# A two-layer encoder trunk: the residual of the feed-forward part moved to DRAM for two of three down products

## The chip, the cores and the metric

The kernel runs on one core of one Trainium2 chip. The metric is the device time of one execution in microseconds (us); lower is better. Three runs of the kernel before gave 1168.78, 1169.61 and 1171.22 us, so the median is 1169.61 us. One more execution was recorded by the hardware profiler, and all rows in this document come from such recorded executions.

## What is computed

Two layers act on a residual stream `x` of 512 tokens by 1024 features, in fp32. Each layer does a token mixer beside a cross-attention, an output projection that is added to `x`, and then the feed-forward part that this change is about:

```python
h = rms_norm(x, ffn_norm[i])
u = h @ w_up                       # 1024 -> 2 * 2816
c = causal_depthwise_conv(u) + b   # width 3
a, g = split(c)
x = x + (silu(g) * a) @ w_down     # 2816 -> 1024
```

The first layer's mixer is differential attention, the second's is a gated linear attention.

## The kernel before, in words

**Layout.** The residual is held transposed: features on the 128 partitions, 512 tokens along the free axis. It has eight tiles `xT[0..7]` of 128x512, stored in pairs as four `xpair` tiles of 128x2x512 in a pool with tag `x2` that has 16 buffers. The same 16 buffers hold the normalised activations `xh`, `xl` (eight pairs: each fp32 operand is split in a rounded high part and a low remainder, and three matmuls take the place of one) and the operands `t1`, `b11` of the down products. Small work tiles of 128x512 come from a second pool with tag `xs` that has five buffers (`xtile()`, line 168).

**Feed-forward part** (`ffn`, line 1106). There are 22 up steps, each of which makes 128 columns of `a` and 128 columns of `g` on TensorE, applies the convolution (ScalarE and VectorE), SiLU (ScalarE) and the product (VectorE), and makes operands of the down product. `GROUPS` = (3, 4, 4) says how many pairs of up steps go into a down product, so the down product is done in three groups; groups one and two stand between up steps, and group three ends the layer. `_ffn()` (line 47) writes this order out: 7 up steps, group one, 8 up steps, group two, 7 up steps, group three.

**A down group** (`down`, line 1154) is written in Strassen's way as 14 products ("steps") with weights `a11`, `s1`, `a12`, `s2`, `s4`, `s3`, `a22` for each of two column halves `c`. A step has 18 matmuls of 128x256 in group one and 24 in the others (3 or 4 blocks, two column tiles, three terms). The result of a step stays in a PSUM bank with tag `lg`, `tp` or `mm` (two banks each), and later steps of the same half go on accumulating in the same bank: `s2`, `s3` and `a22` in the `lg` bank of `a11`, `s4` in the `tp` bank of `s1`. After each step but before the next one in its bank, the bank's content is added to a quarter of the residual: `add(c, tag, f, t)` (line 1176) adds it to the 256 tokens `t` of `xpair[2 * c + f]`. This is one VectorE instruction on 128x512 values, line 1178, that reads PSUM and the residual and writes the residual. Over the 14 adds, the (half, f, t) quarters in order are: c = 0: (0,0), (1,1), (0,0), (0,1), (0,1), (1,1); c = 1: (0,0); c = 0: (1,0); c = 1: (1,1), (0,1), (0,0), (1,1), (0,1), (1,0).

**Weights.** All weights are loaded by SyncE (SP) from one packed tensor into `raw` tiles of which there are six (line 236). ScalarE rounds each to `whi` (line 227 for up weights, 263 for down weights), VectorE subtracts to get `wlo` (lines 230 and 265); there are five buffers of each. VectorE also makes the Strassen sums of the raw down weights (lines 247 to 255). `prefetch` (line 289) keeps the made weights up to five blocks ahead of the matmuls.

**Order of the work.** TensorE follows the order of the program text throughout. Inside a down group ScalarE, VectorE and GpSimd (POOL) follow it too; elsewhere, and for SP always, a scheduler orders the instructions when the kernel is built, by its own forecast of when each is ready. A buffer is given out again when its last reader is done, a DMA included. The kernel reserves 1024 bytes per partition for the descriptors of DMAs that GpSimd issues (line 1337), and issues none from GpSimd in the kernel before. In layer one, the last down group also settles the residual for the next layer and stores it to `xres` in DRAM (line 1239), from which it is read back late in layer two (line 1061); in layer two it stores the output.

Of the kernel before, what the change touches and what calls it, by code (L numbers as in the profile page):

```python
# [11 lines left out]
F32 = mybir.dt.float32  # L12
# [3 lines left out]
ALU = mybir.AluOpType  # L16
# [5 lines left out]
S = 512  # L22
KT = D // 128
# [7 lines left out]
GROUPS = (3, 4, 4)  # L31
X2, XS, EM = 16, 5, 7
# [14 lines left out]
def _ffn():  # L47

    steps, q = [], 0
    for i, nq in enumerate(GROUPS):  # L50
        steps += [("up", t) for t in range(2 * q + (i > 0), 2 * (q + nq) + (i + 1 < len(GROUPS)))]
        steps.append(("down", i))
        q += nq
    return steps
# [96 lines left out]
def trunk(ctx, tc, head_d, x_t, mem_t, wpack, cols_a_d, cols_d, conv_d, gate_d, rel_bias, diff_lambda, consts, onehot, out):  # L151
    nc = tc.nc
    mm = nc.tensor.matmul
    V, A, G = nc.vector, nc.scalar, nc.gpsimd

    perm = ctx.enter_context(tc.tile_pool(name="perm", bufs=1))
    xs = ctx.enter_context(tc.tile_pool(name="xs", bufs=1))
# [3 lines left out]
    dr = ctx.enter_context(tc.tile_pool(name="dr", bufs=1, space=DRAM))  # L161
    ctx.enter_context(tc.manual_schedule(engines={mybir.EngineType.PE}))

    def bank(tag):
        return ps.tile([128, 512], F32, name=f"ps_{tag}", tag=tag)

    def xtile():
        return xs.tile([128, S], F32, name="xt", tag="xs", bufs=XS)
# [14 lines left out]
    def blk(b, w=128):  # L183
        return slice(w * b, w * b + w)
# [13 lines left out]
    def tables(name):  # L198
        tc.keep_in_program_order(A.preload_act_table_set(name))
# [89 lines left out]
    def prefetch(i):  # L289
        size = lambda j: 1 if plan[j][0][0] == "d" else len(blocks[j])  # L290
        by_block = plan[i][0][0] in "ud"
        while len(made) <= i or (len(made) < len(plan) and (
                sum(map(size, range(i, len(made) + 1))) <= WB if by_block else len(made) < i + 2)):
            make_piece()

    def weights(key, more=True):
        i = used[0]
        assert plan[i][0] == key, (plan[i][0], key)
        if more:
            prefetch(i)  # L300
        used[0] += 1
        parts, made[i] = made[i], None
        return parts
# [49 lines left out]
    xT, xpair = [None] * KT, [None] * (KT // 2)  # L353
    xh, xl = [None] * KT, [None] * KT
    xres = dr.tile([KT, 128, S], F32, name="xres")
    bias_d = dr.tile([6, 640], F32, name="bias_d")
    cols_a = perm.tile([128, 32], F32, name="cols_a")
    cols = perm.tile([128, 26], F32, name="cols")
# [76 lines left out]
    with tc.tile_pool(name="ini", bufs=1) as ip, tc.manual_schedule(engines={E.Activation, E.DVE, E.Pool, E.SP}):  # L435
# [7 lines left out]
        p = bank("tp")  # L443
# [662 lines left out]
    def ffn(pool, l, acc):  # L1106
# [47 lines left out]
        def down(g, mids, finish):  # L1154
            last, ks = len(mids) - 1, tuple(range(len(mids)))
            parts, banks, first, last_group = {}, {}, used[0], g + 1 == len(GROUPS)

            def step(c, tag, w, m, ks=ks, start=False, more=True):
                if (c, w) not in parts:
                    parts[c, w] = weights(("d", l, g, c, w), more)  # L1160
                elif more:
                    prefetch(first + more)
                if start:
                    banks[c, tag] = bank(tag)
                p = banks[c, tag]
                hi, lo = parts[c, w]
                for k in ks:
                    mh, ml = mids[k][m]
                    for n in range(2):
                        o, ws = p[:, blk(n, 256)], slice(256 * k + 128 * n, 256 * k + 128 * n + 128)  # L1170
                        terms = (hi, mh), (hi, ml), (lo, mh)
                        for i, (a, b) in enumerate(terms):
                            mm(o[:, ::-1], a[:, ws], b[:, ::-1], start=start and (k, n, i) == (0, 0, 0), stop=k == last and i == 2,  # L1173
                               skip_group_check=True)

            def add(c, tag, f, t):
                x = xpair[2 * c + f][:, :, blk(t, 256)]
                V.tensor_add(x, x, banks[c, tag].rearrange("p (n s) -> p n s", n=2))  # L1178

            def done(c, f, t=None):  # L1180
                for n in range(2):
                    finish(4 * c + 2 * f + n, t)
            if not last_group:
                step(0, "lg", "a11", "b11", start=True)
                add(0, "lg", 0, 0)
                step(0, "tp", "s1", "t1", start=True)
                add(0, "tp", 1, 1)
                step(0, "mm", "a12", "b21", start=True)
                add(0, "mm", 0, 0)
            else:  # L1190
                step(0, "lg", "a11", "b11", ks[:-1], True)
                step(0, "tp", "s1", "t1", ks[:-1], True, False)
                step(0, "mm", "a12", "b21", ks[:-1], True, False)
                step(0, "lg", "a11", "b11", ks[-1:], more=False)
                add(0, "lg", 0, 0)
                step(0, "tp", "s1", "t1", ks[-1:], more=1)
                add(0, "tp", 1, 1)
                step(0, "mm", "a12", "b21", ks[-1:], more=2)
                add(0, "mm", 0, 0)
            step(0, "lg", "s2", "t2")  # L1200
            add(0, "lg", 0, 1)
            step(0, "tp", "s4", "b22")
            add(0, "tp", 0, 1)
            step(0, "lg", "s3", "t3")
            add(0, "lg", 1, 1)
            step(1, "lg", "a11", "b11", start=True)
            add(1, "lg", 0, 0)
            step(0, "lg", "a22", "t4")
            add(0, "lg", 1, 0)
            done(0, 0)  # L1210
            step(1, "tp", "s1", "t1", start=True)
            add(1, "tp", 1, 1)
            step(1, "lg", "s2", "t2")
            add(1, "lg", 0, 1)
            done(0, 1)
            if l == 0 and last_group:
                tables("natural_log_exp_and_others")
            step(1, "mm", "a12", "b21", start=True)
            add(1, "mm", 0, 0)
            done(1, 0, 0)  # L1220
            step(1, "lg", "s3", "t3")
            add(1, "lg", 1, 1)
            done(1, 1, 1)
            step(1, "tp", "s4", "b22")
            add(1, "tp", 0, 1)
            done(1, 0, 1)
            step(1, "lg", "a22", "t4")
            add(1, "lg", 1, 0)
            done(1, 1, 0)
# [11 lines left out]
        def first_steps():  # L1241
            both = [[weights(("u", l, i, h)) for h in range(2)] for i in range(2)]
            banks = [[bank(t) for _ in range(2)] for t in ("mm", "sm")]
            old = list(zip(xh, xl))
            for ks in (K8[:4], K8[4:]):
                for i in range(2):
                    for h in range(2):
                        product(banks[i][h], both[i][h], 0, old, ks)
                        if (i, h, ks[0]) == (0, 1, 0):
                            row_scales(acc[0])  # L1250
                for n in ks[:2]:
                    scaled(n)
                if ks[0]:
                    rows(banks, 0)
                for n in ks[2:]:
                    scaled(n)
            rows(banks, 1)
            return banks
# [6 lines left out]
                banks[i][h] = t[:, blk(h, S)]  # L1265

        opened = None
        for what, i in _ffn():
            if what == "up":
                if i == 0:  # L1270
                    opened = first_steps()
                if i < 2:
                    us = opened[i]
                else:
                    us = [bank("mm" if i % 2 == 0 else "sm") for _ in range(2)]
                    for h in range(2):
                        product(us[h], weights(("u", l, i, h)), 0, list(zip(xh, xl)))
                prefetch(used[0])
                ca = conv(us[0], i)
                cg = conv(us[1], 22 + i)  # L1280
                A.activation(cg, cg, AF.Silu)
                if i % 2 == 0:
                    w = pool.tile([128, 8, 256], F32, name="w", bufs=1)
                    mids.append({})
                V.tensor_mul(w[:, 1 + 2 * (i % 2):3 + 2 * (i % 2)].rearrange("p a b -> p (a b)"), ca, cg)
                middle(i % 2, w, mids[-1])
            else:
                n, last = GROUPS[i], i == len(GROUPS) - 1
                with tc.manual_schedule(engines={E.Activation, E.DVE, E.Pool}):
                    down(i, mids[:n], finish if last else lambda n, t: None)  # L1290
                mids = mids[n:]
# [90 lines left out]
```

## Time and profile before

| what | us |
|---|---|
| median of three runs | 1169.61 |
| the profiled execution, its own time | 1169.78 |
| its span, first to last instruction | 1167.9 |
| TensorE (PE) busy | 1153.8 |
| weight loads into TensorE (PEld) busy | 986.4 |
| VectorE (DVE) busy | 886.4 |
| ScalarE (ACT) busy | 598.9 |
| GpSimd (POOL) busy | 4.1 |

The profiled execution took 1.88 us more than its span. Busy times are sums of the recorded durations of an engine's instructions, overlaps counted once. Matmuls are pipelined, so their recorded durations overlap; how fast TensorE goes is read from the distance of their starts. The feed-forward part of layer one lies at about 256 to 607 us of the span, that of layer two at about 812 to 1168 us. Down groups one and two are at 333 to 363 and 450 to 490 us in layer one and at 890 to 920 and 1007 to 1047 us in layer two.

A row of the table by stages reads: window, its length, then for each engine its busy time and (xcount) of instructions, then the granted TensorE clock as a share of full speed, the mean busy share of the 16 DMA engines, and GB/s moved. A row of a list by source line reads: line, engine, operation, out<-in, count, duration in ns as min/median/max, first and last start. A row of DMA issues reads: out<-in, queue, count, KB each, and the median us from issue to landing. A row of waits reads: who waited <- for whom: us in total, times, the longest. "q" behind an engine's name is its instruction queue, so SPq is SyncE's, which issues DMAs.

### The profile page before, as it was taken

What the parts mean: (1) busy time and instruction counts of PE and PEld (TensorE: products, weight loads), DVE (VectorE), ACT (ScalarE), POOL (GpSimd) and SP (SyncE); (2) the same over time, 40 slices, a digit from 0 to 9 for tenths busy, and PEclk for the clock granted to TensorE, in tenths of its full rate; (3) what the DMA queues carried; (4) which work ended last, traced back from release to release, by engine and by line L of the source; (5) the groups of instructions that cost most, each with busy time, mean ns of one, the idle gap of its engine ahead of it and who ended that gap; (6) DMA issues with size and microseconds to landing.
All of it is one profiled execution on the core that took longest, in us unless ns stands there. A gap on an engine that the chain in (4) does not pass through costs nothing.

```text
span 1167.9 us, 16705 instructions
## 1 busy us (share of the span) xinstructions
PE 1153.8 (99%) x6448; PEld 986.4 (84%) x6448; DVE 886.4 (76%) x1454; ACT 598.9 (51%) x1048; POOL 4.1 (0%) x17
## 2 busy tenths in 40 slices
PE   9999999999999999999999999999999999999998
PEld 6877777788899889988898788988789988998888
DVE  7746677679986778668897746868998777876885
ACT  6847677556443444344467534436654344434441
POOL 0000000000000000000000000000000000000000
PEclk9999999999999999999999999999999999999999
DMA  8533213233126322522253221144222532253212
GB/s 289 176 99 99 68 55 125 61 112 105 63 67 195 91 73 72 163 91 72 66 157 124 73 73 46 47 161 126 86 68 64 183 105 74 73 150 103 72 37 73
DMA packets 39853, 117.94 MB, mean 101 GB/s; under 512 B 4735, under 2 KB 7608, under 8 KB 39774
## 3 DMA queue, kind: packets, MB, share of 16 engines
q1 hardware_dynamic: 39630, 116.62, 32.1%
q8 instruction: 51, 0.84, 0.3%
q10 hardware_dynamic: 144, 0.26, 0.1%
q14 instruction: 28, 0.23, 0.1%
HBM read 112.65 MB, written 4.21 MB: 100 GB/s over the span
## 4 chain that ended last, share of the span: by engine, by line
PE 86%; DVE 8%; ACT 2%; DMA 1%; issue 1%; SPq 0%; DVEq 0%; ACTq 0%
PE ps_mm L348 9%; PE ps_mm L349 9%; PE ps_mm L350 9%; PE ps_lg L1173 8%; PE ps_sm L348 7%; PE ps_sm L350 7%; PE ps_sm L349 7%; PE ps_mm L327 5%; PE ps_mm L329 5%; PE ps_mm L328 5%; PE ps_tp L1173 4%; PE ps_mm L1173 2%; PE ps_tp L196 2%; DVE wlo L265 1%; PE ps_lg L686 1%; PE ps_sm L722 1%
## 5 line engine op out<-in xcount | busy, mean ns | idle before, releaser
L230 DVE TENSOR_TENSOR wlo<-raw,whi 128x1024 fp32r<-128x1024 f32 (+4 forms) x164 | 186.5, 1140 | 86.4 <-ACT whi L227 85.4
L227 ACT CAST whi<-raw 128x1024 fp32r<-128x1024 f32 (+4 forms) x164 | 160.7, 986 | 154.2 <-PE ps_sm L349 69.7
L348 PE MATMUL ps_mm<-x,whi 128*128 128x512 f32 x438 | 172.6, 394 | 0.3 <-DVE midh L1264 0.3
L349 PE MATMUL ps_mm<-x,whi 128*128 128x512 f32 x438 | 170.6, 389 | 0.2 <-DVE x L309 0.2
L350 PE MATMUL ps_mm<-x,wlo 128*128 128x512 f32 x438 | 170.6, 390 | 0.0
L348 PE MATMUL ps_sm<-x,whi 128*128 128x512 f32 x378 | 148.0, 391 | 0.0
L350 PE MATMUL ps_sm<-x,wlo 128*128 128x512 f32 x378 | 147.1, 389 | 0.0
L349 PE MATMUL ps_sm<-x,whi 128*128 128x512 f32 x378 | 147.1, 389 | 0.0
L327 PE MATMUL ps_mm<-whi,x 128*128 128x512 f32 (+2 forms) x336 | 132.0, 393 | 0.0
L329 PE MATMUL ps_mm<-whi,x 128*128 128x512 f32 (+2 forms) x336 | 126.7, 377 | 0.5 <-DVE x L309 0.4
L328 PE MATMUL ps_mm<-wlo,x 128*128 128x512 f32 (+2 forms) x336 | 126.0, 375 | 0.0
L263 ACT CAST whi<-raw 128x1024 fp32r<-128x1024 f32 (+1 forms) x60 | 58.4, 979 | 85.6 <-PE ps_sm L349 26.2
L348 PEld LDWEIGHTS ps_mm<-x,whi 128*128 128x128 f32 x438 | 82.3, 188 | 17.3 <-issue 0.9
L350 PEld LDWEIGHTS ps_mm<-x,wlo 128*128 128x128 f32 x438 | 82.2, 188 | 17.3
L349 PEld LDWEIGHTS ps_mm<-x,whi 128*128 128x128 f32 x438 | 82.3, 188 | 16.9 <-DVE x L309 0.6
L265 DVE TENSOR_TENSOR wlo<-raw,whi 128x1024 fp32r<-128x1024 f32 (+1 forms) x60 | 67.9, 1131 | 24.8 <-ACT whi L263 24.8
L349 PEld LDWEIGHTS ps_sm<-x,whi 128*128 128x128 f32 x378 | 71.0, 188 | 14.9 <-issue 0.5
L348 PEld LDWEIGHTS ps_sm<-x,whi 128*128 128x128 f32 x378 | 71.0, 188 | 14.9 <-issue 0.5
L350 PEld LDWEIGHTS ps_sm<-x,wlo 128*128 128x128 f32 x378 | 71.0, 188 | 14.9
L1173 PE MATMUL ps_lg<-midh,whi 128*128 128x256 f32 x264 | 74.8, 283 | 2.4 <-DVE x L1178 2.4
L1173 PE MATMUL ps_lg<-midh,wlo 128*128 128x256 f32 x264 | 74.3, 282 | 0.0
L1173 PE MATMUL ps_lg<-midl,whi 128*128 128x256 f32 x264 | 74.3, 282 | 0.0
(308 smaller groups left out, 2279.6 us busy)
## 6 DMA issues: line engine op xcount, KB each, us to landing
raw<-in_wpack_dram SPq DMA_DIRECT2D x170, 512.0 KB, 3.6
raw<-in_wpack_dram SPq DMA_DIRECT2D x24, 384.0 KB, 3.1
x<-in_x_t_dram SPq DMA_DIRECT2D x15, 256.0 KB, 5.4
xres<-x SPq DMA_DIRECT2D x8, 256.0 KB, 3.7
x<-xres SPq DMA_DIRECT2D x8, 256.0 KB, 4.6
raw<-in_wpack_dram SPq DMA_DIRECT2D x7, 256.0 KB, 6.7
bt<-bias_d SPq DMA_DIRECT2D x6, 256.0 KB, 5.1
x<-in_mem_t_dram SPq DMA_DIRECT2D x4, 256.0 KB, 6.0
```

What stands on the lines that cost most here:

```text
L196: nc.tensor.transpose(dst, src, ident[:n, :n])
L227: ins = A.copy(hi[:, c], raw[:, c])
L230: V.tensor_sub(lo[:, c], raw[:, c], hi[:, c].bitcast(F32))
L263: A.copy(hi[:, c], raw[:, c])
L265: todo = [lambda: V.tensor_sub(lo[:, c], raw[:, c], hi[:, c].bitcast(F32)), lambda: [sum_weights((*key[:3], *x)) for x in after]]
L327: mm(p, sh[k][:, blk(b)], hi, start=k == 0, stop=False)
L328: mm(p, sh[k][:, blk(b)], lo, start=False, stop=False)
L329: mm(p, sl[k][:, blk(b)], hi, start=False, stop=k == KT - 1)
L348: mm(p, hi[:, blk(n)], bh, start=i == first, stop=False)
L349: mm(p, hi[:, blk(n)], bl, start=False, stop=False)
L350: mm(p, lo[:, blk(n)], bh, start=False, stop=i == last)
L1173: mm(o[:, ::-1], a[:, ws], b[:, ::-1], start=start and (k, n, i) == (0, 0, 0), stop=k == last and i == 2, skip_group_check=True)
```

## The change

A DRAM copy `xacc[l]` of the residual is added for each layer. When the feed-forward part begins, SP writes the four `xpair` tiles to it, 512 KB each. In down groups one and two the VectorE add goes away: ScalarE copies the PSUM bank into an `xs` tile, and a DMA issued by GpSimd adds that tile to the quarter of `xacc[l]` in DRAM (`accum_op=add`, 256 KB, in rows of 1 KB). Before up step 17, the third after down group two, four new `xpair` tiles are taken and SP reads the accumulated residual back into them. Group three adds to them on VectorE as before. No line is removed from the rest of the kernel.

```diff
     xres = dr.tile([KT, 128, S], F32, name="xres")
+    xacc = [dr.tile([KT // 2, 128, 2, S], F32, name=f"xacc{l}") for l in range(2)]
...
             def add(c, tag, f, t):
-                x = xpair[2 * c + f][:, :, blk(t, 256)]
-                V.tensor_add(x, x, banks[c, tag].rearrange("p (n s) -> p n s", n=2))
+                pv = banks[c, tag].rearrange("p (n s) -> p n s", n=2)
+                if last_group:
+                    x = xpair[2 * c + f][:, :, blk(t, 256)]
+                    V.tensor_add(x, x, pv)
+                    return
+                y = xtile().rearrange("p (n s) -> p n s", n=2)
+                A.copy(y, pv)
+                G.dma_start(xacc[l][2 * c + f][:, :, blk(t, 256)], y, accum_op=ALU.add)
...
         opened = None
+        for n in range(KT // 2):
+            nc.sync.dma_start(xacc[l][n], xpair[n])
         for what, i in _ffn():
             if what == "up":
                 if i == 0:
                     opened = first_steps()
+                if i == sum(GROUPS[:-1]) * 2 + 3:
+                    for n in range(KT // 2):
+                        xpair[n] = xs.tile([128, 2, S], F32, name="x2", tag="x2", bufs=X2)
+                        nc.sync.dma_start(xpair[n], xacc[l][n])
+                        xT[2 * n], xT[2 * n + 1] = xpair[n][:, 0], xpair[n][:, 1]
```

## The prediction, made before the changed kernel was run

> **What bounds the kernel now.** I read the page first, then the table by stages for the feed-forward parts, then who TensorE waits for.
>
> ```profile
> span 1167.9 us, 16705 instructions
> PE 1153.8 (99%) x6448; PEld 986.4 (84%) x6448; DVE 886.4 (76%) x1454; ACT 598.9 (51%) x1048; POOL 4.1 (0%) x17
> ```
>
> ```profile
> core 0: us, PE busy (x) PEld busy (x) DVE busy (x) ACT busy (x) POOL busy (x), PEclk, DMA share, GB/s
> 262.00:333.00 71.00, 71.00 (x314) 58.60 (x313) 64.52 (x92) 38.09 (x53) 0.00 (x0) 1.00 0.25 76
> 333.00:363.00 30.00, 29.84 (x251) 29.64 (x250) 27.44 (x36) 14.16 (x17) 0.00 (x0) 1.00 0.51 156
> 363.00:450.00 87.00, 87.00 (x387) 72.10 (x386) 63.03 (x81) 38.00 (x49) 0.00 (x0) 1.00 0.30 90
> 450.00:490.00 40.00, 40.00 (x339) 39.92 (x338) 33.20 (x37) 16.47 (x17) 0.00 (x0) 1.00 0.43 132
> 490.00:567.00 77.00, 77.00 (x346) 63.90 (x345) 54.66 (x69) 33.42 (x43) 0.00 (x0) 1.00 0.28 83
> 817.00:890.00 73.00, 72.65 (x320) 59.50 (x319) 65.25 (x92) 39.60 (x55) 0.00 (x0) 1.00 0.24 68
> 890.00:920.00 30.00, 30.00 (x254) 29.92 (x253) 27.84 (x36) 14.08 (x18) 0.00 (x0) 1.00 0.51 160
> 920.00:1007.00 87.00, 87.00 (x386) 72.05 (x385) 63.03 (x81) 38.09 (x50) 0.00 (x0) 1.00 0.29 89
> 1007.00:1047.00 40.00, 40.00 (x339) 39.96 (x338) 32.91 (x38) 16.60 (x18) 0.00 (x0) 1.00 0.44 132
> 1047.00:1124.00 77.00, 77.00 (x346) 63.96 (x345) 54.63 (x70) 33.57 (x44) 0.00 (x0) 1.00 0.27 82
> ```
>
> TensorE is the bound, at full clock: in the stages that the change touches it is idle 0.16 us (333 to 363) and 0.35 us (817 to 890), 0.51 us in all. VectorE looks heavy in the first group (27.44 of 30 us), but whether that costs anything is read from the waits. The first row below is the whole kernel, the second the same view for 329 to 363 us.
>
> ```profile
> PE ps_lg L1173 <- DVE x L1178: 2.4, 4, 1.0
> ```
>
> ```profile
> PE ps_lg L1173 <- DVE x L1178: 0.2, 1, 0.2
> ```
>
> Of the 2.4 us that matmuls waited for the residual adds, 0.2 us lie in a group that is changed. So whatever VectorE is spared here can return about half a microsecond, and the question is what the new path costs.
>
> **The change part by part.** *The adds leave VectorE, copies come to ScalarE.* The rows of the add, then the nearest row of the copy (ScalarE, PSUM to SBUF, same shape):
>
> ```profile
> L1178 DVE TENSOR_TENSOR x<-x,ps_lg x48: 675/680/689, 335.3 to 1164.0; 128x512 f32<-128x512 f32 x48
> L1178 DVE TENSOR_TENSOR x<-x,ps_tp x24: 676/680/689, 338.1 to 1161.2; 128x512 f32<-128x512 f32 x24
> L1178 DVE TENSOR_TENSOR x<-x,ps_mm x12: 675/680/689, 340.5 to 1155.5; 128x512 f32<-128x512 f32 x12
> ```
>
> ```profile
> L606 ACT COPY em<-ps_tp x4: 568/586/593, 136.5 to 187.9; 128x512 f32<-128x512 f32 x4
> ```
>
> The 84 adds are six groups of 14; four groups change, so 56 adds go: 56 x 0.68 = 38 us off VectorE, none of it on the path. Onto ScalarE come 56 x 0.586 = 33 us: per group 14 x 0.586 = 8.2 us, so 14.16 + 8.2 = 22.4 of 30 us in group one and 24.7 of 40 in group two. Is each copy in time? The chain of work shows how long a step is (18 matmuls in group one, 24 in group two):
>
> ```profile
> 350.66 2.13 PE ps_tp L1173 x18
> ...
> 456.17 2.84 PE ps_mm L1173 x24
> ```
>
> A bank is needed again one step after the step that filled it (the `s3` step after `s4`), so a copy may come 2.13 - 0.6 = 1.5 us late in group one. Ahead of it on ScalarE stands one weight cast per step, 0.83 us by the rows below, and 0.83 + 0.59 is under 2.13.
>
> ```profile
> 342.11 0.84 ACT L263 CAST whi<-raws 128x768 fp32r<-128x768 f32 x1 [1.64 <-DVE raws L247]
> 345.72 0.83 ACT L263 CAST whi<-raws 128x768 fp32r<-128x768 f32 x1 [2.77 <-DVE raws L250]
> ```
>
> The cast that waits longest (2.77 us for a Strassen sum) ends at 346.55; the step whose copy stands behind it ends at about 345.9, so that copy is some 0.7 us late, inside the 1.5 us; and VectorE, without its adds, makes the sum sooner. I cost this part at nothing; if that cover went, it is some 0.7 us per such cast.
>
> *The accumulating transfers.* This is the term that decides. Each of the 56 copies is followed by a 256 KB transfer that GpSimd issues; the `xs` tile is free again when it has landed, and there are five tiles. Two transfers to one quarter of the residual may not overlap, so by the order of the quarters transfer 3 waits for 1, 5 for 4, 6 for 2, 11 for 7, 12 for 9, 13 for 10; GpSimd issues in order, so what waits holds back all transfers behind it. The trace has no transfer issued by GpSimd and no accumulating one. The nearest rows are SP's writes and reads of the same 256 KB, and how long SP is busy issuing one:
>
> ```profile
> xres<-x SPq DMA_DIRECT2D x8, 256.0 KB, 3.7
> x<-xres SPq DMA_DIRECT2D x8, 256.0 KB, 4.6
> ```
>
> ```profile
> L1239 SPq DMA_DIRECT2D xres<-x x8: 319/375/432, 584.5 to 612.9; - x8
> ```
>
> An accumulation has to read DRAM and write it. From below, it is as quick as the read alone, 4.6 us; from above, it is read and write one after the other, 4.6 + 3.7 = 8.3 us. The middle is 6.45. For GpSimd's issue I take twice SP's 0.38, c = 0.8 us (an estimate; SP's own value is the lower end, one step of 2.13 us the upper, where GpSimd itself would set the pace). So X = 7.2 us from a finished copy to its landing. Then in group one, with time zero at the start of its first step:
>
> - copy 1 is done at 2.13 + 0.6 = 2.7, its transfer lands at 9.9; transfer 3 has been ready since 7.0 and is issued at 9.9;
> - transfer 4, ready at 9.1, goes out behind it at 10.7 and lands at 17.9; transfer 5 goes to the same quarter, is issued at 17.9 and lands at 25.1, which is 2.7 + 3X + c;
> - copy 10 is the first to need the tile of copy 5. It could begin at 10 x 2.13 = 21.3, begins at 25.1 and ends at 25.7. Step 12 needs that bank at 11 x 2.13 = 23.4: **TensorE waits 2.3 us**.
>
> In group two a step is 2.84 us: copy 1 is done at 3.4, transfer 3 goes at 10.6, transfer 4 (ready at 12.0) at 12.0, 5 at 19.2, landing at 26.4; copy 10 is due at 28.4. No wait. So the sum is 2 layers x 2.3 = 4.6 us. At X = 4.6 it is zero, at 8.3 it is 2 x 5.6 = 11.2, and the wait begins at X = 6.4.
>
> The Trainium skill, "DMA: Bandwidth & Descriptors", section "Anatomy of one DMA — SWDGE (gpsimd) path", fits a transfer issued by GpSimd as about 2.0 us plus the bytes over 436 GB/s; for 256 KB that is an estimate of 2.6 us, and by it the sum would be zero. [...]
>
> *The load on the DMA engines* speaks for the upper half of X:
>
> ```profile
> q1 hardware_dynamic: 39630, 116.62, 32.1%
> ```
>
> 116.62 MB took 32.1% of 1167.9 us, 375 us, so 0.84 us of all 16 engines per 256 KB. Fourteen transfers are 12 us if an accumulation costs as much as a copy, 24 us if twice as much. In group one the engines are busy 0.51 x 30 = 15 us already: 27 to 39 of 30 us.
>
> *The writes at the start* (SP, 4 x 512 KB per layer): 2 MB are 6.7 us of transfer ahead of some up weights. What hides them is that weights are loaded far ahead: SP's loads wait for VectorE to free a raw tile, and the casts there wait for TensorE to free their output, not for a load.
>
> ```profile
> SPq L236 <- DVE wlo L230: 526.0, 124, 25.7
> ```
>
> ```profile
> 270.38 1.06 ACT L227 CAST whi<-raw 128x1024 fp32r<-128x1024 f32 x1 [1.68 <-PE ps_mm L349]
> ...
> 275.82 1.06 ACT L227 CAST whi<-raw 128x1024 fp32r<-128x1024 f32 x1 [1.66 <-PE ps_sm L349]
> ```
>
> Cost nothing; without the cover up to 6.7 us a layer. *The reads back* stand in SP's queue and wait for the last transfers of group two, which land some 8 us after it; weight loads behind them wait as long. Group three begins 77 us after group two, and six raw and five cast tiles stand ahead of TensorE, at over 5 us each (24 matmuls of an up weight). Cost nothing, at most the same 6.7 us.
>
> **Sum.** 1169.78 (the profiled execution, 1.88 above its span) - 0 + 4.6 = 1174.4 us. That execution is 0.17 above the median of the runs, which changes nothing.
>
> **The rivals.** *All hidden.* X stays under 6.4 us: the transfers lag, no copy waits for a tile, and the time is 1169.8. For it: a plain 256 KB transfer of the tile `xres` can land in 2.0 us, the smallest value in the view of that tile, and a read and a write at that pace are 4.0 us. TensorE then has at most the 0.5 us from above to win.
>
> ```profile
> DMA to landing us min/median/max: 2.0/4.3/5.6
> ```
>
> *One transfer at a time.* If only one accumulation can be in flight, be it that the 1024 bytes of line 1337 hold the descriptors of one only, or that every write to `xacc` is held to be in conflict with the one before, the 14 go in single file. Copy 12 then needs the tile of copy 7, which lands at 2.7 + 7 x 7.2 = 53.1; step 14 needs its bank at 13 x 2.13 = 27.7, so 26.0 us are lost in group one with the copy itself, and 17.5 in group two: 87 us in all, 1257 us. It costs from X = 3.5 us on (2.7 + 7X + 0.6 = 27.7); at X = 4.6 it is 16 us. Against the conflict: two writes of neighbouring columns of one DRAM tile were issued 0.4 us apart, while transfers of that tile take 3.1 us or more to land.
>
> ```profile
> L501 SPq DMA_DIRECT2D bias_d<-x x2: 286/288/289, 25.6 to 26.0; - x2
> ...
> DMA to landing us min/median/max: 3.1/5.1/7.1
> ```
>
> The Trainium skill, "SBUF — State Buffer", section "SBUF size: 192, 224, or 256?", lists 16 KiB per partition as the usual room for these descriptors, sixteen times what is reserved here; no run so far shows how many transfers fit.
>
> *Faster.* VectorE, less loaded, lets all 2.4 us of the waits for adds go, also in the third groups, whose adds stay: 1167.4. Only 0.2 us of it is where the change acts, so this needs a luckier order from the scheduler.
>
> *ScalarE cannot keep up, or the copies come in another order than I think.* Casts and copies then delay each other, some 0.7 us per group and more: 1173 to 1180. Its busy time in the groups (22.4 of 30) speaks against it.
>
> **How the numbers follow.** The case of my sum, X from 6.8 to about 9, has a chance of 0.42, its own range is 1172 to 1186; all hidden 0.38; one at a time 0.12; ScalarE 0.03; faster 0.05. A change of 0.2%, 2.3 us, is about what a measurement of this kernel can tell from none. Faster 0.05, same 0.38, slower 0.42 + 0.12 + 0.03 = 0.57. The range leaves out most of "one at a time" and of "faster": 1167.5 to 1188.
>
> **What would show it.** Right: waits of TensorE for ScalarE's copies in the later steps of group one, ScalarE's copies waiting for a DMA, GpSimd waiting for landings at transfers 3 and 5, landings of 6 to 8 us after the issue, no wait in group two. Wrong: landings under 6 us with TensorE idle as little as now (hidden); every transfer issued only when the last has landed (one at a time); weight casts that wait for loads at the start of the feed-forward part or behind the reads (the covers of SP's transfers gone); less than 2 us of idle TensorE gone elsewhere (faster).

## The result and the profile after

The changed kernel took 1211.26 us (median of 4 runs, 1206.74 to 1213.97); the kernel before took 1169.68 us in the same comparison (4 runs). The ratio is 1.035, with an interval of [1.0316, 1.0384]: some 41 us slower, above the whole range of the prediction. The profiled execution of the changed kernel took 1210.51 us.

First the page of the changed kernel: the span, the engines' busy times, the queue of GpSimd's transfers (packets, MB, share), and the new transfers (count, KB, median us from issue to landing).

```profile
span 1208.6 us, 16899 instructions
...
PE 1163.6 (96%) x6448; PEld 994.4 (82%) x6448; DVE 854.2 (71%) x1398; ACT 626.7 (52%) x1104; POOL 66.0 (5%) x73
...
q0 software_dynamic: 15232, 14.68, 9.7%
...
xacc<-xt POOLq DMA_DIRECT2D x56, 256.0 KB, 4.8
...
x<-xacc SPq DMA_DIRECT2D x8, 512.0 KB, 3.9
```

The span grew by 40.7 us. TensorE does the same 6448 matmuls, is busy 9.8 us longer (1163.6 against 1153.8) and idle 30.9 us longer (1208.6 - 1163.6 = 45.0 against 14.1). These two parts are the whole difference. VectorE is 32.2 us less busy and ScalarE 27.8 us more (copies overlap the casts behind them, and overlaps count once); neither shows in the time.

Who TensorE waits for, the two largest rows of the whole changed kernel (us in total, times, longest):

```profile
PE ps_lg L1174 <- ACT xt L1184: 30.1, 8, 8.1
PE ps_lg L1174 <- DVE x L1181: 2.4, 3, 1.0
```

The first row is new and is the idle part: 30.1 of 30.9 us. The second is the wait for the residual adds, and it is 2.4 us as before. The lines have moved: L1174 is the matmul of a down step, L1184 ScalarE's copy, L1185 GpSimd's transfer. The eight waits, from the timeline of TensorE (in brackets the idle time in front of the matmul and who ended it):

```profile
364.86 0.58 PE L1174 MATMUL ps_lg<-midh,whi 128*128 128x256 f32 x1 [8.15 <-ACT xt L1184]
...
374.68 0.39 PE L1174 MATMUL ps_lg<-midh,whi 128*128 128x256 f32 x1 [3.03 <-ACT xt L1184]
...
495.96 0.39 PE L1174 MATMUL ps_lg<-midh,whi 128*128 128x256 f32 x1 [0.60 <-ACT xt L1184]
...
505.87 0.39 PE L1174 MATMUL ps_lg<-midh,whi 128*128 128x256 f32 x1 [3.96 <-ACT xt L1184]
...
939.64 0.58 PE L1174 MATMUL ps_lg<-midh,whi 128*128 128x256 f32 x1 [5.73 <-ACT xt L1184]
...
949.82 0.39 PE L1174 MATMUL ps_lg<-midh,whi 128*128 128x256 f32 x1 [3.99 <-ACT xt L1184]
...
1072.64 0.39 PE L1174 MATMUL ps_lg<-midh,whi 128*128 128x256 f32 x1 [0.58 <-ACT xt L1184]
...
1082.66 0.39 PE L1174 MATMUL ps_lg<-midh,whi 128*128 128x256 f32 x1 [4.08 <-ACT xt L1184]
```

Each group has two, ahead of step 12 and of step 14: the steps that need a `lg` bank whose content ScalarE hasn't yet copied out. In group one they come to 11.2 and 9.7 us, in group two to 4.6 and 4.7.

ScalarE itself is not slow. Its timeline in group one of layer one, copies alone:

```profile
350.40 0.59 ACT L1184 COPY xt<-ps_lg 128x512 f32<-128x512 f32 x1 [0.81 <-PE ps_lg L1174]
...
359.31 0.59 ACT L1184 COPY xt<-ps_tp 128x512 f32<-128x512 f32 x1 [7.59 <-DMA xacc<-xt]
...
364.22 0.59 ACT L1184 COPY xt<-ps_lg 128x512 f32<-128x512 f32 x1 [3.60 <-DMA xacc<-xt]
...
374.04 0.59 ACT L1184 COPY xt<-ps_lg 128x512 f32<-128x512 f32 x1 [3.63 <-DMA xacc<-xt]
```

Up to copy 8 (350.40) a copy waits for its step. Copy 9 is the first to wait for a landed transfer, because it needs the tile of copy 4; copy 10 (364.22) holds step 12, and copy 12 (374.04) holds step 14. So the five `xs` tiles run out. Why, is seen on GpSimd, in the timeline of the same group:

```profile
336.35 1.21 POOL L1185 DMA_DIRECT2D xacc<-xt  x1 [150.87 <-ACT xt L1184]
341.03 1.13 POOL L1185 DMA_DIRECT2D xacc<-xt  x1 [3.46 <-ACT whi L263]
345.59 1.10 POOL L1185 DMA_DIRECT2D xacc<-xt  x1 [3.43 <-issue]
350.26 1.11 POOL L1185 DMA_DIRECT2D xacc<-xt  x1 [3.57 <-ACT whi L263]
359.83 1.10 POOL L1185 DMA_DIRECT2D xacc<-xt  x1 [8.46 <-DMA xacc<-xt]
364.43 1.11 POOL L1185 DMA_DIRECT2D xacc<-xt  x1 [3.50 <-issue]
369.09 1.10 POOL L1185 DMA_DIRECT2D xacc<-xt  x1 [3.55 <-issue]
```

Copies are made every 2.13 us, transfers go out every 4.6 or 4.7 us, and once after 9.6. Transfers 2, 4, 6 and 7 go to quarters that nothing in flight touches and their copies are long done, yet each leaves some 0.3 us after the one before it has landed. In all four groups no transfer was issued while another was in flight. The wait is booked as "issue", which is time in which an engine waits for nothing that the profile shows; where a cast (`whi`) is named, it ended by chance at that moment, since the transfer doesn't read it. Over all of the kernel the rows of waits give POOL 31 such stalls with 122.6 us.

Last, the 9.8 us by which TensorE is longer busy. The table by stages around the wait at 356.7 to 364.9 us, then the four other stretches in which the granted clock was at half:

```profile
core 0: us, PE busy (x) PEld busy (x) DVE busy (x) ACT busy (x) POOL busy (x), PEclk, DMA share, GB/s
356.30:359.70 3.40, 0.41 (x4) 0.20 (x2) 0.00 (x0) 0.40 (x1) 0.00 (x0) 1.00 0.28 90
359.70:369.90 10.20, 5.04 (x23) 5.05 (x24) 2.18 (x2) 3.48 (x6) 3.02 (x3) 0.50 0.75 139
...
506.50:509.90 3.40, 3.40 (x18) 3.40 (x18) 1.23 (x1) 0.26 (x1) 0.05 (x1) 0.50 0.91 106
936.50:943.30 6.80, 3.66 (x17) 3.66 (x18) 1.23 (x1) 1.53 (x2) 1.09 (x1) 0.50 0.81 161
950.20:953.60 3.40, 3.40 (x19) 3.40 (x18) 1.23 (x1) 0.51 (x1) 0.29 (x1) 0.50 0.89 128
1083.30:1086.70 3.40, 3.40 (x18) 3.40 (x18) 1.23 (x1) 0.26 (x1) 0.04 (x1) 0.50 0.87 112
```

The column PEclk drops to 0.50 during or right after the waits of about 4 us and more, and matmuls then start every 0.213 us instead of every 0.118 (the distances of their starts in the timeline). Some 88 matmuls started in these stretches: 88 x 0.095 = 8.4 us, an estimate. So of the 40.7 us, 30.1 are waits for copies, and 8 to 9 are what the half clock after these waits cost.

### The profile page after: what moved, and what is told of

Read it like the earlier page. It is cut to its first block, busy times and chain, and to the rows that moved or that the text cites. A ratio compares the mean times of both kernels' runs of the same rounds, so it can differ in the third digit from the quotient of the medians.

```text
span 1208.6 us, 16899 instructions
## 1 busy us (share of the span) xinstructions
PE 1163.6 (96%) x6448; PEld 994.4 (82%) x6448; DVE 854.2 (71%) x1398; ACT 626.7 (52%) x1104; POOL 66.0 (5%) x73
## 3 DMA queue, kind: packets, MB, share of 16 engines
q0 software_dynamic: 15232, 14.68, 9.7%
## 5 line engine op out<-in xcount | busy, mean ns | idle before, releaser
L1174 PE MATMUL ps_lg<-midh,whi 128*128 128x256 f32 x264 | 79.1, 300 | 32.6 <-ACT xt L1184 30.1
L1185 POOL DMA_DIRECT2D xacc<-xt x56 | 61.9, 1105 | 766.4 <-ACT xt L1184 560.7
L349 PEld LDWEIGHTS ps_mm<-x,whi 128*128 128x128 f32 x438 | 82.3, 188 | 16.9 <-DVE x L309 0.6
L1174 PEld LDWEIGHTS ps_lg<-midh,whi 128*128 128x128 f32 x264 | 53.5, 203 | 34.7 <-ACT xt L1184 31.8
```

What stands on the lines that cost most here:

```text
L349: mm(p, hi[:, blk(n)], bl, start=False, stop=False)
L1185: G.dma_start(xacc[l][2 * c + f][:, :, blk(t, 256)], y, accum_op=ALU.add)
```

## The experiments

**The theory** after this reading: the 1024 bytes that the kernel reserves for the descriptors of GpSimd's DMAs hold those of one accumulating transfer, so GpSimd can't write the next before the last has landed; single file at 5 us, against a copy every 2.13 or 2.84 us, empties the five tiles. **Rivals**: the writes to `xacc` are held to be in conflict with each other, whatever the room; accumulating transfers are simply too slow for the DMA engines, and would be with more of them in flight; or part of the loss comes from SP's writes and reads or from ScalarE's copies.

### More room for descriptors, and what it costs

The buffers fill SBUF, so the room has to come from somewhere: here one of the seven `em` buffers.

```diff
-X2, XS, EM = 16, 5, 7
+X2, XS, EM = 16, 5, 6
...
-... dynamic_dma_scratch_size=1024)
+... dynamic_dma_scratch_size=3072)
```

> The changed kernel with 3072 bytes per partition instead of 1024 for the descriptors of GpSimd's transfers (and, to make room, six instead of seven em tiles in layer one's attention). Theory A, the room for descriptors holds one accumulating transfer at a time: several are now in flight, GpSimd issues one about 1.1 to 2.2 us after another wherever the program has no wait, TensorE's waits for ScalarE's copies fall from 30.1 us to under 6 us, the granted clock is 1.0 in the down groups, time 1168 to 1178 us. Theory B, accumulating transfers go one after another whatever the room (the DMA engines or the conflict rule of the program): each is still issued 0.3 us after the landing of the one before, waits stay at about 30 us, time 1205 to 1215 us.

It took 1180.02 us (4 runs) against 1168.97 of the kernel before: ratio 1.0086 [1.007, 1.0103]. Rows of its waits and of its DMA issues, then GpSimd's timeline in group one:

```profile
PE ps_lg L1174 <- ACT xt L1184: 4.0, 3, 2.2
...
POOL xacc L1185 <- issue: 4.4, 2, 2.8
...
xacc<-xt POOLq DMA_DIRECT2D x56, 256.0 KB, 7.7
```

```profile
342.00 1.21 POOL L1185 DMA_DIRECT2D xacc<-xt  x1 [155.76 <-ACT xt L1184]
344.11 1.10 POOL L1185 DMA_DIRECT2D xacc<-xt  x1 [0.90 <-ACT xt L1184]
347.15 2.29 POOL L1185 DMA_DIRECT2D xacc<-xt  x2 [1.94 <-ACT whi L263]
355.60 5.58 POOL L1185 DMA_DIRECT2D xacc<-xt  x5 [6.16 <-ACT whi L263]
```

Transfers now go out in packs (x2, x5), a good microsecond apart, while one takes 7.7 us to land; up to five are in flight at a time. GpSimd's stalls for nothing shown fall from 122.6 to 4.4 us, and TensorE's waits for copies from 30.1 to 4.0 us. Nothing about the order or the destinations was altered, so conflicts between the writes don't hold them: the room does. The waits came out as expected, the time and the clock did not: 1180.02 us is above the 1168 to 1178 expected, and the granted clock was 0.50 twice, for 6.8 us from 185.71, in layer one's attention, from which the buffer was taken, and for 3.4 us from 922.98, at the end of the wait of 2.2 us. So the price of the buffer was measured by itself, on the kernel before.

```diff
-X2, XS, EM = 16, 5, 7
+X2, XS, EM = 16, 5, 6
```

> The kernel before with six instead of seven em tiles in layer one's attention, the price of the room that the run with 3072 bytes had to make. That run reached its first up steps 5.8 us later than the changed kernel, so 1173 to 1177 us; if it comes out at 1169 us, those microseconds came from the room itself.

1173.31 us (5 runs) against 1169.07, ratio 1.0038 [1.0025, 1.0051]: the buffer costs 4.2 us. If the two add up, which wasn't tried, the room alone would leave 1180.0 - 4.2 = 1175.8 us. The profiled executions of the two kernels with six buffers differ by 9.1 us in span (1179.5 against 1170.4): 4.0 of them are the waits for copies, and 4.2 are a longer busy TensorE (1159.0 against 1154.8), which goes with the two stretches at half clock; the kernel before with six buffers had none in its profiled execution.

### More tiles, the same room

Every second copy takes a tile of the pool `x2`, so that about nine are in turn.

```diff
-                y = xtile().rearrange("p (n s) -> p n s", n=2)
+                turn[0] += 1
+                y = (pair()[0] if turn[0] % 2 == 0 else xtile()).rearrange("p (n s) -> p n s", n=2)
```

> The changed kernel, but every second copy of ScalarE goes to a tile of the pool with 16 buffers, of which four are free once the residual is in DRAM, so about nine tiles instead of five are there for copies; the room for descriptors stays 1024 bytes. If the loss is the wait for a free tile behind transfers in single file: transfers stay in single file, about 5 us apart, copy 12 of group one needs the tile of about transfer 3 or 4 (landed by 23 us, the copy is due at 26 us), no copy waits for a landing for more than about 2 us, and the time is 1168 to 1176 us. If single file hurts in another way (GpSimd, the weight loads beside it, the clock): TensorE still waits 15 us or more, time over 1185 us.

1174.41 us (4 runs), ratio 1.0046 [1.0031, 1.0061]. Its rows of waits:

```profile
PE ps_lg L1174 <- DVE x L1181: 3.5, 3, 1.6
PE ps_lg L1174 <- ACT x L1185: 1.4, 2, 1.0
...
POOL xacc L1186 <- issue: 127.2, 27, 7.7
```

GpSimd stalls as long as in the changed kernel (127.2 us): still single file. Four copies, late ones of their groups, waited 3.8 to 8.2 us for a landing, more than the 2 us expected, but TensorE waits for copies only 1.4 us and its clock stays at 1.00. So most of the loss needs both, single file and tiles that run out before the 14 transfers of a group have caught up. Single file isn't shown to be free: this kernel is still 5.4 us slower than the one before, clear of the noise. Of the 3.7 us by which the span is longer than before (1171.6), the rows name 1.4 and the 1.1 more that is waited for adds in the third groups.

### Plain writes in place of accumulating ones

```diff
-                G.dma_start(xacc[l][2 * c + f][:, :, blk(t, 256)], y, accum_op=ALU.add)
+                G.dma_start(xacc[l][2 * c + f][:, :, blk(t, 256)], y)
```

The sums of groups one and two are left out here: each write overwrites the quarter.

> The changed kernel with plain instead of accumulating transfers from GpSimd, everything else the same, 1024 bytes of room (the sums in DRAM are overwritten instead of added to). If an accumulating transfer takes about twice the descriptors of a plain one, two or three plain ones fit and overlap, the issues are 1 to 3 us apart where the program has no wait, a landing comes 3 to 4 us after the issue, and the time is 1168 to 1180 us. If any transfer by GpSimd goes in single file: issues 4 us apart and more, time over 1190 us.

One run: 1170.85 us. The queue's row, the landing, GpSimd's stalls, and three rows of its timeline:

```profile
q0 software_dynamic: 4480, 14.68, 3.3%
...
xacc<-xt POOLq DMA_DIRECT2D x56, 256.0 KB, 4.2
...
POOL xacc L1185 <- issue: 6.6, 3, 3.3
```

```profile
348.56 1.40 POOL L1185 DMA_DIRECT2D xacc<-xt  x2 [3.76 <-ACT xt L1184]
350.52 0.69 POOL L1185 DMA_DIRECT2D xacc<-xt  x1 [0.57 <-ACT xt L1184]
352.66 0.70 POOL L1185 DMA_DIRECT2D xacc<-xt  x1 [1.44 <-ACT xt L1184]
```

The same 14.68 MB go to the same places, with the same 1024 bytes, in 4480 packets instead of 15232: 80 for a transfer instead of 272. Landing takes 4.2 us, hardly less than 4.8, but the transfers follow their copies at 2.13 us, up to three in flight at a time. So it is not the landing time that sets the pace; it is how many are let in flight. Nothing but the kind of the transfer differs, so the destinations as such don't hold the writes one by one; that the room does it, and not the accumulation by itself, is shown by the run with 3072 bytes. That an accumulating transfer fills the room with its larger number of descriptors is inferred from the packets; the descriptors themselves aren't in the trace.

### Smaller transfers, and both remedies together

The same room, but each accumulation in two parts of 128 KB, in one kernel with five tiles and in another with about nine (as above). All sums are kept.

```diff
-                G.dma_start(xacc[l][2 * c + f][:, :, blk(t, 256)], y, accum_op=ALU.add)
+                for n in range(2):
+                    G.dma_start(xacc[l][2 * c + f][:, n, blk(t, 256)], y[:, n], accum_op=ALU.add)
```

> The changed kernel with each accumulating transfer issued as two of 128 KB (one per feature tile of the pair), 1024 bytes of room as in the change, all sums kept. Theory A, the room for descriptors decides: a whole transfer leaves no room for a second one, so two or three halves fit; halves of one copy overlap, a copy's tile is free every 2.5 to 4 us instead of every 5 us, TensorE's waits for copies fall from 30.1 us to under 10 us, time 1169 to 1184 us. Theory B, transfers go in single file whatever their size: two issues of about 1 us and two landings of 3 us or more per copy, 8 us per copy, waits over 70 us, time over 1250 us.

1182.95 us (4 runs) against 1169.07, ratio 1.0106 [1.0078, 1.0134].

```profile
PE ps_lg L1174 <- ACT xt L1184: 9.1, 4, 4.5
...
POOL xacc L1186 <- issue: 62.2, 43, 3.6
```

```profile
343.23 2.66 POOL L1186 DMA_DIRECT2D xacc<-xt  x3 [2.45 <-ACT whi L263]
...
353.18 1.75 POOL L1186 DMA_DIRECT2D xacc<-xt  x2 [2.46 <-DMA xacc<-xt]
```

With halves, two or three go out one behind the other (x3 at 343.23, x2 at 353.18), and up to three are in flight at a time, never more, although GpSimd's total issue time is longer: an issue takes 0.88 us, and there are twice as many. The stalls halve and TensorE's waits fall from 30.1 to 9.1 us. As in the changed kernel, the rest of the loss is a longer busy TensorE: 1157.9 us, 4.1 more than before.

> Both remedies together: halves of 128 KB and about nine tiles for the copies. By theory A neither room nor tiles are awaited, TensorE waits for a copy less than 1 us in all, and the time is 1169 to 1173 us: no better than the kernel before, since TensorE had only 0.5 us to win in these stages. By theory B (single file whatever the size): over 1200 us.

1168.49 us (10 runs), ratio 0.9997 [0.9987, 1.0006]. Its page, and the first row of its waits:

```profile
PE 1153.0 (99%) x6448; PEld 986.1 (85%) x6448; DVE 854.3 (73%) x1398; ACT 626.2 (54%) x1104; POOL 103.2 (9%) x129
```

```profile
PE ps_lg L1174 <- DVE x L1181: 2.3, 3, 1.0
```

No wait of TensorE for copies is left and the clock is 1.00 throughout. GpSimd still stalls 52.5 us for nothing shown, so the room is still waited for, other than expected; the nine tiles cover it. This is the whole change with its loss removed, VectorE as lightly loaded as in the changed kernel (854.3 us), and the time is that of the kernel before. So there was nothing to win: an interval of 0.9987 to 1.0006 leaves room for 1.5 us at most. No version that beats the kernel before came out of these runs.

### The other parts alone

SP's writes and reads alone (VectorE adds as before, to the old tiles, which the reads then replace, so the sums of groups one and two are left out):

```diff
-                y = xtile().rearrange("p (n s) -> p n s", n=2)
-                A.copy(y, pv)
-                G.dma_start(xacc[l][2 * c + f][:, :, blk(t, 256)], y, accum_op=ALU.add)
+                x = xpair[2 * c + f][:, :, blk(t, 256)]
+                V.tensor_add(x, x, pv)
```

> Only SP's part of the change: the residual is written to DRAM at the start and read back before up step 17, the adds of groups one and two stay on VectorE and go to the old tiles (so they are left out of what is read back; no copy by ScalarE, no transfer by GpSimd). If these transfers are hidden, as I costed them: 1168 to 1171 us. If they hold up weight loads: up to 6.7 us a layer each, 1173 to 1195 us, with weight casts that wait for loads.

1169.0 us (10 runs) against 1168.97, ratio 1.0 [0.999, 1.0009]. And everything but GpSimd's transfers, whose sums are again left out:

```diff
                 A.copy(y, pv)
-                G.dma_start(xacc[l][2 * c + f][:, :, blk(t, 256)], y, accum_op=ALU.add)
```

> The changed kernel without GpSimd's transfers: ScalarE's copies, the writes at the start and the reads back stay, the sums of groups one and two are left out. If copies, queue order and SP's part are hidden as I costed them: 1168 to 1171 us, no wait of TensorE for a copy above 0.3 us. If ScalarE's queue is late by itself: some 0.7 us per group and more, 1172 to 1180 us.

1168.85 us (10 runs) against 1169.07, ratio 0.9998 [0.9989, 1.0008]. The copies from the `lg` banks in layer one's group one (333 to 363 us), from its list by source line (count, busy us, mean ns, idle time in front of them):

```profile
L1184 ACT COPY xt<-ps_lg 128x512 f32<-128x512 f32 x7 | 4.1, 588 | 4.8 <-PE ps_lg L1174 4.7
```

Copies wait for matmuls here, and no matmul for a copy. Neither part explains any of the 41 us beyond the noise of about 1 us: the loss comes with the accumulating transfers.

## Why the prediction was wrong, step by step

- **What bounds the kernel: right.** TensorE was the bound, and VectorE's 32 us less bought nothing (the kernel of halves with nine tiles).
- **Copies on ScalarE: right**, at 0.59 us each and no cost (copies alone).
- **SP's writes and reads: right**, no cost (SP's part alone). The reads landed in 6.4 us at the median there and in 3.9 in the changed kernel, both far inside the cover.
- **The step that failed: "transfer 4, ready at 9.1, goes out behind it at 10.7".** The prediction let GpSimd issue whenever its last issue was over and no transfer to the same quarter was in flight. In the changed kernel each transfer waited for the landing of the one before: transfer 2 went out at 341.03, 0.3 us after transfer 1 had landed, though its copy was done at 338.16, and transfer 4 at 350.26, 0.3 us after transfer 3 had landed. That is about 16.9 us into the group instead of 10.7 (an estimate, with the start of the group 2.7 us before the end of the first copy, at 336.03). This is the rival "one transfer at a time", with the reason it named first, the 1024 bytes. It had a chance of 0.12, and most of it lay outside the range.
- **Its price was too high for another reason.** The 7.2 us from copy to landing are near what transfers took that shared the DMA engines (7.7 us at the median with more room, 4.3 to 13.4 us), not for single file: there a landing took 4.8 us at the median, and with some 0.3 us to the next issue the pace is about 5.1. The rival's own formula, with this pace put in after the fact, then gives 2.7 + 35.7 + 0.6 - 27.7 = 11.3 us for group one and 3.4 + 35.7 + 0.6 - 36.9 = 2.8 for group two, 28.2 us in all; measured were 11.2 and 9.7, 4.6 and 4.7, together 30.1. What is over lies in the second groups, where the fourth and the fifth transfer were late: in layer one, transfers 4, 5 and 6 went out at 482.58, 489.11 and 495.54 us.
- **The half clock after waits was in no case.** It made 30 us of waits into some 39.
- **Where the first wait appears was right**: five tiles, copy 10 held by transfer 5, step 12 held by copy 10. The waits ahead of step 14, and those in group two, were not in the sum. With room for several transfers the forecast's mechanism is what happened: step 12 of the first groups waited 0.93 us in layer one and 2.20 us in layer two, against 2.3 forecast for each. A wait of 0.83 us ahead of step 14 came on top, so that the total of 4.0 us lies so near the forecast 4.6 is in part luck.
- **The estimate of 2.6 us** for a transfer of 256 KB issued by GpSimd was met by the fastest of the plain ones alone (2.5 us); their median was 4.2, and the accumulating ones of the changed kernel took 4.3 us and more.

The mistake can be named more exactly. Against single file the prediction had two plain writes 0.4 us apart on SP's queue. They were of 12 and 3 KB, and the 3.1 us set beside them are of reads of the same tile: the writes have no landing on record, so it isn't shown that they overlapped. And what holds on SP's queue was carried to GpSimd's, whose transfers need the room that the kernel reserves for them. No row of the trace of before could have shown how many fit, since GpSimd issued nothing there; seen from the result, the one figure that was at hand, 1024 bytes, deserved more than 0.12 against a change that sends 56 accumulating transfers through it.

## What to carry to other kernels

Before work is moved to GpSimd's DMAs, ask how many of these transfers can be in flight, and compare landing time over that number with the pace of the producer; the number of buffers behind the producer only says how long a mismatch stays hidden. In these profiles a full descriptor room shows as GpSimd waiting for nothing, with each issue right behind a landing. Taking work from an engine that nobody waits for wins nothing, and a stall of a few microseconds on TensorE may cost up to a third more than itself.

## What the runs showed of the hardware

- **Half clock after a stall.** After waits of 3.96 to 8.15 us TensorE was granted 0.50 of its clock, in stretches of 3.4 us or two or three times that (6.8, 10.2). The 3.03 us wait at 374.68 was followed by full clock, and one of 2.20 us, with more room for descriptors, by half clock (its first matmul, at 923.28, took 0.58 us instead of 0.39, and PEclk is 0.54 over the next 3.4 us). The Trainium skill, "TensorE: Matmul & The Clock Gate", section "The HAM clock gate (the "warmup" mystery)", says that the clock is set by how busy TensorE was in free-running windows of 3413 ns, and halved after at least one idle window. The lengths of the stretches agree. A halving after 2.20 us of idleness doesn't, if the window has to be idle as a whole; the measurement decides. Laid end to end from the changes of the clock, the stretch from 369.93 to 373.34 has TensorE busy for 1.72 of its 3.41 us and was followed by full clock; the one from 919.57 to 922.98, with more room, has it busy for 1.51 us and was followed by half. The wait of 3.03 us was spread over two such stretches, which would explain why it had no such effect; a rule isn't shown by two cases.
- **An accumulating transfer is a different thing from a plain one of the same size**: 272 packets against 80, 1.10 us of GpSimd's time against 0.69, one in flight in 1024 bytes against up to three. Its landing took 4.8 us at the median in single file, the plain one's 4.2 with others beside it, and its own 7.7 with others beside it.
- **Open**: how many bytes of the room one accumulating transfer takes (an estimate, if each keeps its part until it has landed: in 1024 bytes there were never two in flight, in 3072 up to five, so more than 512 and at most some 610), why single transfers land late (transfer 4 of layer one's first group took 9 us), and where the smaller rest of the nine-tile kernel's 5.4 us comes from.
